# Mixer: residual base moved behind the scan and onto VectorE, out projection summed once; attention: the context's query and key norm moved ahead

## The chip, the cores and the metric

The kernel runs on one core of a Trainium2 chip. The metric is device time in microseconds (us) of one execution, the median of several runs. PE is TensorE, PEld its weight loads, DVE is VectorE, ACT ScalarE, POOL GpSimd and SP SyncE, which issues most DMAs.

## What is computed

The reference runs two networks of depth 2 on 512 tokens of width 1024, in fp32. The first one has in each layer a SwiGLU feed-forward net (FFN), a mixer and a second FFN; the second one has attention (grouped-query in layer 0, latent attention in layer 1, both with a context of 256 tokens) and an MLP. Cut to the parts that the change touches:

```
# mixer of layer l: three groups side by side, one out projection, a residual with layer norm
proj = h @ mix_w_in[l]                      # h = modulated x
y_ssd = mamba2_group(...)                   # 512 wide: conv, chunked scan, gate, group RMS norm
y_fox = fox_group(...)                      # 256 wide: forgetting attention
y_sc  = shortconv_group(...)                # 256 wide
y = concat([y_ssd, y_fox, y_sc]) @ mix_w_out[l]
x = layer_norm(ALPHA * x + gate * y, ln_g, ln_b)
# grouped-query attention: queries and keys of context and latents
q, k, v = split(h @ w_qkv)
q = rms_norm(q, q_norm); k = rms_norm(k, k_norm)    # the latents also get rope
```

## The kernel before

Tokens lie on the partitions for residuals (`z`, two tiles of 128 x 2 x 1024) and features on the partitions for what feeds a product. Every product is made of three fp32r matmuls on high and low parts (`mm3`): a value x is split into `hi` (cast by ACT) and `lo = x - hi` (DVE, or POOL where a piece of the plan says so). `WeightStream.fetch` (L288 to L304) loads a 512 KB block to one of three `raw` buffers by a DMA on SP, casts `hi` on ACT and subtracts `lo` on DVE, or in halves on POOL for the blocks in `onpool`. The blocks are taken in the order of `plan()`; at most five split pairs exist, three are fetched ahead, and a block in `extra` gets a place in the FFN's pool.

The tile framework simulates a timeline and orders each engine's instructions by it, with the order of the program as priority; on the chip every engine then runs its list in order. SBUF pools of consecutive phases share addresses: the mixer's pool `mx` and the attention's `gq` take the place of the FFN pool (`ff`), tile by tile as old tiles are released. PSUM has eight banks: tags "a" (two tiles of one bank), "b" (two tiles of two), "c" and "d" (one each).

**Mixer.** `mixer()` projects and convolves (`conv`, tiles `pxb` and `pxs`), and after the first four blocks calls `put_by`: that loads the layer norm's rows, lets POOL form the next residual base `ALPHA * (z * g + b)` in 4 scalings and 16 tensor operations of 128x512 (`next_base(..., True)`, L585 to L592) and then stores `z` to DRAM (`keep`). The scan and the forgetting attention follow. `out_first` (= `scan_out`) loads the base back and, while the gates, the short convolution and the group norm are computed, multiplies the FOX half `yq[0][:, 0:2]` by the first two blocks of `mo`, adding the gated result to `z` for each of eight 128x512 parts (L652, L654). After the mixer a phase with the FFN pool opens, and `out_chunk` multiplies the remaining 768 rows by six blocks and adds again, with the row sums for the layer norm (L652, L657). The low parts of all eight `mo` blocks are made by POOL.

**Attention.** `gqa_first` multiplies the context by the first four blocks of `w_qkv` while the norm of the latents still runs; its results stay in PSUM. In `gqa()` the generator `steps()` of head group 0 copies them to `gq`, takes squares, sums, `rsqrt`, gain (`norm(0)`), splits (`st`), transposes them (`turn`, tile `ptq`) and goes on with the projection of the latents (`dense(1, 0)`, `dense(1, 1)`, and so on), interleaved with the context's four heads.

Of the kernel before, what the change touches and what calls it, by code (L numbers as in the profile page):

```python
# [10 lines left out]
F32 = mybir.dt.float32  # L11
# [264 lines left out]
class WeightStream:  # L276
# [8 lines left out]
    def fetch(self):  # L285
        nc = self.nc
        src = self.plan[self.issued]
        n = src.shape[-1]  # L288
        self.issued += 1
        raw = self.pool.tile([P, DM], F32, tag="raw", bufs=self.raw_bufs, name="raw")  # L290
        if self.issued - 1 in self.extra:
            hi, lo = (self.extra_pool().tile([P, DM], F32R, tag="w" + i, bufs=1, name="w" + i) for i in "hl")
# [19 lines left out]
class Kernel:  # L312
# [526 lines left out]

    def mixer(self, l, h, put_by, out_first):  # L840
        nc, tc, ws = self.nc, self.tc, self.ws
        tt, stt, ts = nc.vector.tensor_tensor, nc.vector.scalar_tensor_tensor, nc.vector.tensor_scalar
        with tc.tile_pool(name="mx", bufs=1, reuse_waits="tile") as mp:
# [33 lines left out]

            put_by(lambda: T("le", 4, name="gb"))

# [291 lines left out]
    def softmax(self, ps, pool, pn, turn):  # L1171
# [100 lines left out]
    def gqa_first(self, hc):  # L1272

        w = [self.ws.next() for _ in range(4)]
        pb = self.ps("b", [P, CTB, SEQ], "pqkv")
        ps = [pb[:, tb, :384] for tb in range(CTB)]
        for tb in range(CTB):
            self.dense_tok(ps[tb], w, 2, 384, hc, range(KT), tb)
        return w, ps

    def gqa(self, h, hc, first, out_first):
# [4 lines left out]
        with tc.tile_pool(name="gq", bufs=1, reuse_waits="tile") as gp:  # L1286
# [4 lines left out]
            gain = gain[:, None].broadcast_to([P, 2, 5, 64])  # L1291
            yfc = self.xpool.tile([P, KT, CTX], F32, tag="lb", bufs=1, name="yfc")

            work = []

# [5 lines left out]
            def project(g):  # L1301
# [9 lines left out]

                def dense(b, i):
                    src, tb = (hc, 0) if b == 0 else (h, 2 * b - 2)
                    if i == 0:
                        tiles[b] = T("x", (P, 2, 5, 64)), T("t2", (P, 2, 5, 64))
                    x, sq = tiles[b]
                    v = out["v"][:, 2 * b + i]
                    if g == 0 and b == 0:
                        ps = first[1][i]
                    else:  # L1320
                        ps = self.ps("a" if g == 0 else "d", [P, 384], "pqkv")
                        self.dense_tok(ps, out["w"], 2, 384, src, range(KT), tb + i)
                    p5 = ps[:, 0:320].rearrange("p (h e) -> p h e", h=5)
# [3 lines left out]

                def norm(b):
                    x, sq = tiles[b]
                    tb = 2 * b - 2  # L1330
# [6 lines left out]
                    x10 = x.rearrange("p t h e -> p (t h) e")  # L1337
                    tt(x10, x10, r[:, :, None].broadcast_to([P, 10, 64]), op=ALU.mult)
                    st = tiles[b] = T("st", (P, 2, 6, P), 1, F32R)
                    dup = lambda i: st[:, :, i].rearrange("p t (a e) -> p t a e", a=2)  # L1340
# [19 lines left out]
                def steps():  # L1360
                    for b in range(3):
                        dense(b, 0)
# [16 lines left out]
            def head(g, q, out, ctx):  # L1379
# [9 lines left out]
                j = 2 * g + q // 2  # L1389
                return score, out["v"], yfc[:, j] if ctx else yf[j // 4][:, j % 4], (q % 2) * 64, t, nkb  # L1390

            def context_out(i):
                y = self.quads(1, CTX, "yc")[0]
                for j in range(4):
                    self.split(y[0][:, j], y[1][:, j], yfc[:, 4 * i + j], i == 0)
                return y

            def heads():
                out, steps = project(0)
                work.append(steps)  # L1400
                fill(6)
                for q in range(4):
# [195 lines left out]
    def plan(self):  # L1598
# [16 lines left out]
        def wide():  # L1615

            self.ws.extra.add(len(p))
# [15 lines left out]
        for l in range(DEPTH):  # L1633
# [21 lines left out]
    def run(self):  # L1655
        nc, tc, d = self.nc, self.tc, self.d
        with ExitStack() as es:
# [27 lines left out]
            self.ws = WeightStream(tc, wp, ahead=3, split_bufs=5, raw_bufs=3)  # L1685
            self.ws.extra_pool = lambda: self.fpool
            self.plan()
# [75 lines left out]
            for l in range(DEPTH):  # L1763
# [14 lines left out]

                def put_by(rows):

                    for n in range(2):
                        f = slice(n * SEQ, n * SEQ + SEQ)
                        gb = [rows(), rows()]
                        for i, x in enumerate(gb):
                            nc.sync.dma_start(x, d["rows"][1 + 3 * l, i][:, f])
                        self.next_base(old, SEQ, gb, f, True)
                    kept.append(keep(old))

                def scan_out(y, space):
                    z.extend(self.load_rows(kept[0], "z"))  # L1790
                    yield
                    self.ws.ahead = 2
                    gate = self.row(m1(1, 2), "c", space)
                    yield from self.out_steps([(z, gate, [y], SEQ)], (2,))

                yo, ys = self.mixer(l, h, put_by, scan_out)
# [4 lines left out]
                gate = self.row(m1(1, 2), "c")  # L1801
                self.out_chunk([(z, gate, [[a[:, 2:4] for a in yo], ys], SEQ)], (2, 4), True)
                h = norm(z, self.sums[0], SEQ, 2 + l * 3, m1(2, 0), m1(2, 1), 1e-5, f"md{l}1")
# [96 lines left out]
```

## Time and profile before

| | us |
|---|---|
| median of 3 runs | 3837.87 (3837.38 to 3838.32) |
| the profiled execution, its own time | 3839.17 |
| span of the profiled execution, first to last instruction | 3837.3 |
| TensorE busy within the span | 3637.5 (95%) |
| VectorE busy | 2529.1 (66%) |
| ScalarE busy | 1534.4 (40%) |
| GpSimd busy | 359.3 (9%) |
[...]

Two executions of the kernel before differ by up to some 0.02%. Busy times are unions over the instructions of an engine; a matmul's row shows more than its pace, since the next one starts before it ends. The mixer of layer 0 lies at some 412 to 640 us of the span and that of layer 1 at 1430 to 1650 us, the start of the grouped-query attention at 2045 to 2120 us.

### The profile page before, as it was taken

Reading aid. Unit: us, or ns where it says so; the run is one execution under the profiler, and the core shown is the slowest. Engines: PE = TensorE matmul, PEld = TensorE weight load, DVE = VectorE, ACT = ScalarE, POOL = GpSimd, SP = SyncE. Lnnn points to the kernel's source line nnn. Section 1 sums busy time; section 2 is a strip of 40 time slices with the busy share of each in tenths; the row PEclk is TensorE's granted clock in tenths of the full one; section 3 lists DMA queues with packets and bytes.
Section 4 is the critical chain, followed back from the end, with each engine's and each line's share of the span. In section 5 each row is a group of like instructions: output and inputs, shape, how many; then the busy total and the mean of one; then the engine's idle time right before and its main releaser. Section 6 shows DMA issues by size and latency. Waiting matters only on the chain. (4 is left out here: it accounts for less than half of the span.)

```text
span 3837.3 us, 49056 instructions
## 1 busy us (share of the span) xinstructions
PE 3637.5 (95%) x18970; PEld 3077.3 (80%) x18970; DVE 2529.1 (66%) x4245; ACT 1534.4 (40%) x2748; POOL 359.3 (9%) x388
## 2 busy tenths in 40 slices
PE   6999999999999999999998898999999979989998
PEld 5888777888888887778887787788888878878887
DVE  8775665777777966579665778664444558776454
ACT  3222443422332234452224566443232457644333
POOL 0000323000000004310001115100000001130000
PEclk9999999999999999999999899999999989999999
DMA  7663322566446633235642001122221210112222
GB/s 289 213 195 119 106 71 99 167 206 208 158 160 198 208 105 111 71 122 186 208 154 72 21 23 67 35 61 66 66 62 55 77 37 30 41 55 91 95 94 66
DMA packets 121738, 428.77 MB, mean 112 GB/s; under 512 B 13656, under 2 KB 19672, under 8 KB 119072
## 3 DMA queue, kind: packets, MB, share of 16 engines
q1 hardware_dynamic: 119584, 421.44, 33.7%
q10 hardware_dynamic: 1920, 4.19, 0.3%
q8 instruction: 149, 2.44, 0.3%
q14 instruction: 85, 0.70, 0.1%
HBM read 415.10 MB, written 10.49 MB: 111 GB/s over the span
## 5 line engine op out<-in xcount | busy, mean ns | idle before, releaser
L296 ACT CAST hi<-raw 128x1024 fp32r<-128x1024 f32 (+2 forms) x502 | 518.4, 1035 | 1314.4 <-PE pgu L348 726.6
L301 DVE TENSOR_TENSOR lo<-raw,hi 128x1024 fp32r<-128x1024 f32 (+2 forms) x472 | 577.0, 1224 | 337.5 <-ACT hi L296 333.8
L348 PE MATMUL pgu<-hl,hi 128*128 128x512 f32 (+1 forms) x1536 | 567.7, 370 | 4.5 <-DVE hl L530 2.9
L347 PE MATMUL pgu<-hh,hi 128*128 128x512 f32 (+1 forms) x1536 | 565.8, 370 | 5.7 <-ACT hh L621 3.3
L349 PE MATMUL pgu<-hh,lo 128*128 128x512 f32 (+1 forms) x1536 | 566.4, 369 | 0.0
L652 DVE TENSOR_TENSOR po<-po,gate 128x512 f32<-128x512 f32 x376 | 259.0, 696 | 357.6 <-PE po L349 357.6
L347 PE MATMUL po<-hi,gh 128*128 128x512 f32 x1216 | 474.4, 391 | 5.6 <-DVE z L654 3.1
L348 PE MATMUL po<-lo,gh 128*128 128x512 f32 x1216 | 472.8, 390 | 0.0
L349 PE MATMUL po<-hi,gl 128*128 128x512 f32 x1216 | 468.0, 389 | 0.0
L463 DVE SCALAR_TENSOR_TENSOR amul<-araw,crow 128x1024 f32<-128x1024 f32 x288 | 351.4, 1220 | 31.5 <-DMA araw<-in_ada 30.1
L348 PEld LDWEIGHTS pgu<-hl,hi 128*128 128x128 f32 x1536 | 292.8, 191 | 54.0 <-DVE hl L530 3.5
L347 PEld LDWEIGHTS pgu<-hh,hi 128*128 128x128 f32 x1536 | 291.4, 191 | 54.2 <-ACT hh L621 3.7
L349 PEld LDWEIGHTS pgu<-hh,lo 128*128 128x128 f32 x1536 | 292.9, 191 | 47.6 <-DVE lo L301 0.3
L347 PEld LDWEIGHTS po<-hi,gh 128*128 128x128 f32 x1216 | 228.4, 188 | 55.3 <-DVE z L654 5.6
L349 PEld LDWEIGHTS po<-hi,gl 128*128 128x128 f32 x1216 | 228.2, 188 | 47.8
L348 PEld LDWEIGHTS po<-lo,gh 128*128 128x128 f32 x1216 | 228.5, 188 | 45.1
L564 POOL TENSOR_TENSOR st<-st,mhalf 128x2 f32<-128x2 f32 (+2 forms) x24 | 19.9, 828 | 2601.9 <-DVE st L563 2601.9
L348 PE MATMUL pm<-hl,hi 128*128 128x512 f32 (+1 forms) x576 | 210.2, 366 | 2.0 <-DVE hl L622 2.0
L347 PE MATMUL pm<-hh,hi 128*128 128x512 f32 (+1 forms) x576 | 210.3, 367 | 1.9 <-ACT hh L621 1.6
L654 DVE TENSOR_TENSOR z<-po,z 128x512 f32<-128x512 f32 x304 | 206.5, 687 | 5.1
L349 PE MATMUL pm<-hh,lo 128*128 128x512 f32 (+1 forms) x576 | 209.5, 364 | 0.2 <-DVE lo L301 0.2
L333 DVE TENSOR_TENSOR gl<-gf,gh 128x512 fp32r<-128x512 f32 (+1 forms) x158 | 105.3, 668 | 115.7 <-ACT gh L331 115.0
(468 smaller groups left out, 7090.9 us busy)
## 6 DMA issues: line engine op xcount, KB each, us to landing
araw<-in_ada SPq DMA_DIRECT2D x224, 512.0 KB, 4.4
raw<-in_w SPq DMA_DIRECT2D x128, 512.0 KB, 3.5
raw<-in_f1i SPq DMA_DIRECT2D x88, 512.0 KB, 4.2
raw<-in_f2i SPq DMA_DIRECT2D x88, 512.0 KB, 3.8
raw<-in_mi SPq DMA_DIRECT2D x48, 512.0 KB, 3.5
raw<-in_f1o SPq DMA_DIRECT2D x44, 512.0 KB, 4.2
raw<-in_f2o SPq DMA_DIRECT2D x44, 512.0 KB, 4.4
arawf<-in_ada SPq DMA_DIRECT2D x16, 512.0 KB, 9.0
```

The costliest lines, as they stand in the source:

```text
L296: nc.scalar.copy(hi[:, :n], raw[:, :n])
L301: self.lo = nc.vector.tensor_tensor(lo[:, :n], raw[:, :n], hi[:, :n].bitcast(F32), op=ALU.subtract)
L333: ins = eng.tensor_tensor(lo, src, hi.bitcast(F32), op=ALU.subtract)
L347: mm(ps, ah, bh, start=start and i == 0, stop=False)
L348: mm(ps, ah, bl, start=False, stop=False)
L349: mm(ps, al, bh, start=False, stop=stop and i == n - 1)
L463: ins = nc.vector.scalar_tensor_tensor(m, w, 1.0, row, op0=ALU.mult, op1=ALU.mult, accum_out=res[:, j : j + 1])
L564: nc.gpsimd.tensor_tensor(r, sq, self.mhalf[:, :n], op=ALU.pow)
L652: nc.vector.tensor_tensor(ps, ps, gate[:, f], op=ALU.mult)
L654: nc.vector.tensor_tensor(to, ps, zf, op=ALU.add)
```

## The change

1. `put_by` now only stores `z`. `take_back`, called after the scan, loads `z` and four row tiles (in the scan's `le` buffers) and forms the base on DVE, in 16 operations of 128x512.
2. `out_first`, its gate row and its eight gated additions go. A new `mixer_out` multiplies all eight `mo` blocks into one accumulation for each of the eight parts: six parts (tags "b" and "a") take the FOX and short convolution halves, then each part its SSD half; the last two take everything after that. One gated addition each.
3. The low parts of the `mo` blocks and of four 128x512 pieces of `yq[0]` move from POOL to DVE. Blocks 4 to 7 of `mo` all get places in the FFN pool (tag "q4").
4. The short convolution's split now stands behind the group norms', whose four splits follow their own group.
5. `gqa_first` copies the context's queries and keys out of PSUM and norms them there, in the free tile `room`; `steps()` of group 0 is written out anew: the context's split, both projections of the first latent half, the context's transposes, and the products of the second half before its copies.

```diff
-    def mixer(self, l, h, put_by, out_first):
+    def mixer(self, l, h, put_by, take_back):
...
-            put_by(lambda: T("le", 4, name="gb"))
+            put_by()
...
-            work = out_first([a[:, 0:2] for a in yq[0]], T("vt", shape=(P, DM), name="gate"))
-            next(work)
+            base = take_back(lambda: T("le", 4, name="gb"))
+            next(base)
...
-                eng = nc.vector if g else nc.gpsimd
-                eng.tensor_tensor(lo, x, hi.bitcast(F32), op=ALU.subtract)
+                nc.vector.tensor_tensor(lo, x, hi.bitcast(F32), op=ALU.subtract)
...
-            group_norm(0)
-            group_norm(1)
+            yq += self.quads(1, SEQ, "my")
+            for g in range(2):
+                group_norm(g)
+                for j in range(2 * g, 2 * g + 2):
+                    split(1, j, xs[j])
             for j in range(2):
                 split(0, 2 + j, tmp[j])
-            yq += self.quads(1, SEQ, "my")
-            for j in range(4):
-                split(1, j, xs[j])
-            for _ in work:
+            for _ in base:
                 pass
+    def mixer_out(self, z, gate, yo, ys):
...
+        for part in range(2):
+            w += [self.ws.next() for _ in range(2)]
+            for tb, n in list(ps):
+                products(tb, n, part)
+        w += [self.ws.next() for _ in range(4)]
+        gate = self.row(gate, "c")
+        for tb in range(NTB):
+            for n in range(2):
+                if tb == NTB - 1:
+                    ps[tb, n] = self.ps("a", [P, SEQ], "po")
+                for part in range(0 if tb == NTB - 1 else 2, 4):
+                    products(tb, n, part)
...
+                nc.vector.tensor_tensor(p, p, gate[:, f], op=ALU.mult)
+                nc.vector.scalar_tensor_tensor(
+                    x, p, 1.0, x, op0=ALU.mult, op1=ALU.add, accum_out=self.sums[0][:, tb, n : n + 1]
+                )
...
     def gqa_first(self, hc):
...
+        x, sq = (cut(i * 640, i * 640 + 640).rearrange("p (t h e) -> p t h e", t=2, h=5) for i in range(2))
+        gain = cut(1280, 1600)
+        self.nc.sync.dma_start(gain, self.d["gqa_g"])
         for tb in range(CTB):
             self.dense_tok(ps[tb], w, 2, 384, hc, range(KT), tb)
+            p5 = ps[tb][:, 0:320].rearrange("p (h e) -> p h e", h=5)
+            self.nc.scalar.copy(x[:, tb], p5)
+            self.nc.scalar.activation(sq[:, tb], p5, AF.Square)
+        self.head_norm(x, sq, gain.rearrange("p (h e) -> p h e", h=5), lambda i: cut(1600 + 16 * i, 1610 + 16 * i))
...
+                    if g == 0:
+                        take(0, 0)
+                        take(0, 1)
+                        norm(0)
+                        dense(1, 0)
+                        dense(1, 1)
+                        for i in (2, 0, 1):
+                            turn(0, i)
+                        product(2, 0)
+                        product(2, 1)
+                        yield
+                        norm(1)
...
-            onpool(0, 8)
-            p.extend(d["mo"][l, i] for i in range(4))
-            wide()
-            p.extend(d["mo"][l, i] for i in range(4, 8))
+            for i in range(8):
+                if i > 3:
+                    wide()
+                p.append(d["mo"][l, i])
...
+                def take_back(rows):
...
+                    for n in range(2):
+                        for i in range(2):
+                            nc.sync.dma_start(gb[n][i], d["rows"][1 + 3 * l, i][:, n * SEQ : n * SEQ + SEQ])
+                    yield
...
+                            nc.vector.scalar_tensor_tensor(x, x, ALPHA, gb[n][0], op0=ALU.mult, op1=ALU.mult)
+                            nc.vector.scalar_tensor_tensor(x, gb[n][1], ALPHA, x, op0=ALU.mult, op1=ALU.add)
```

## Rows read from the trace of the kernel before

**Rows 1.** The page, busy time and share of the span.

```profile
PE 3637.5 (95%) x18970; PEld 3077.3 (80%) x18970; DVE 2529.1 (66%) x4245; ACT 1534.4 (40%) x2748; POOL 359.3 (9%) x388
```

**Rows 2.** Waits of PE, 405 to 700 us: total, times, longest.

```profile
PE pxs L347 <- ACT xbc L868: 4.5, 1, 4.5
```

**Rows 3.** Waits of PE, 1440 to 1720 us.

```profile
PE pxs L347 <- ACT xbc L868: 5.9, 1, 5.9
```

**Rows 4.** Timeline of DVE before the first wait: start, duration, instruction.

```profile
452.71 1.94 DVE L301 TENSOR_TENSOR lo<-raw,hi 128x1024 fp32r<-128x1024 f32 x1
...
454.81 1.07 DVE L907 TENSOR_TENSOR u<-u,sgn 128x48 f32<-128x48 f32 x1
455.91 1.20 DVE L908 SCALAR_TENSOR_TENSOR e<-u 128x48 f32<-128x48 f32 x1
457.14 0.19 DVE L919 TENSOR_SCALAR u<-u 128x48 f32<-128x48 f32 x1
```

**Rows 5.** Timeline of POOL, 423 to 462 us, its last row.

```profile
444.04 13.00 POOL L592 TENSOR_TENSOR z<-z,gb 128x512 f32<-128x512 f32 x8
```

**Rows 6.** Groups of DVE by line, 700 to 1000 us: busy, mean ns.

```profile
L301 DVE TENSOR_TENSOR lo<-raw,hi 128x1024 fp32r<-128x1024 f32 x56 | 68.4, 1222 | 37.4 <-ACT hi L296 37.4
```

**Rows 7.** Groups of DVE by line, 1446 to 1471 us.

```profile
L919 DVE TENSOR_SCALAR u<-u 128x48 f32<-128x48 f32 x1 | 1.2, 1165 | 0.0
```

**Rows 8.** Stretches: length, busy PE, PEld, DVE, ACT, POOL, PEclk, DMA.

```profile
461.40:466.70 5.30, 5.29 (x13) 4.14 (x14) 3.75 (x5) 1.89 (x3) 0.00 (x0) 0.50 0.47 116
...
1470.40:1474.00 3.60, 3.58 (x9) 2.88 (x10) 3.53 (x5) 1.27 (x2) 3.03 (x2) 0.53 0.20 26
622.50:638.90 16.40, 9.84 (x38) 5.98 (x36) 14.65 (x21) 5.34 (x8) 7.62 (x5) 1.00 0.22 64
...
1632.20:1648.50 16.30, 9.79 (x38) 5.96 (x36) 14.55 (x21) 5.29 (x8) 7.64 (x5) 1.00 0.20 63
...
588.00:622.50 34.50, 34.50 (x155) 27.84 (x154) 15.04 (x14) 15.92 (x23) 18.64 (x13) 1.00 0.20 63
```

**Rows 9.** Groups by line and shape, the whole span.

```profile
L652 DVE TENSOR_TENSOR po<-po,gate 128x512 f32<-128x512 f32 x376 | 259.0, 696 | 357.6 <-PE po L349 357.6
...
L654 DVE TENSOR_TENSOR z<-po,z 128x512 f32<-128x512 f32 x304 | 206.5, 687 | 5.1
...
L333 DVE TENSOR_TENSOR gl<-gf,gh 128x512 fp32r<-128x512 f32 x146 | 100.3, 688 | 113.2 <-ACT gh L331 113.1
```

**Rows 10.** Timeline of PE in the out projection: starts show the pace.

```profile
640.68 0.40 PE L348 MATMUL po<-lo,myh 128*128 128x512 f32 x1
640.91 0.39 PE L349 MATMUL po<-hi,myl 128*128 128x512 f32 x1
```

**Rows 11.** Timeline of ACT, 620 to 652 us.

```profile
634.61 1.14 ACT L1148 CAST myh<-xbc 128x512 fp32r<-128x512 f32 x2
...
645.30 1.05 ACT L296 CAST wh<-raw 128x1024 fp32r<-128x1024 f32 x1
```

**Rows 12.** Timeline of PE at the attention's start, 2074 to 2090 us.

```profile
2076.66 0.33 PE L348 MATMUL pqkv<-lo,hh 128*128 128x384 f32 x1
2076.84 0.33 PE L349 MATMUL pqkv<-hi,hl 128*128 128x384 f32 x1
...
2086.41 1.15 PE L1350 MATMUL ptq<-ident,st 128*128 128x128 f32 x4 [7.85 <-ACT st L331]
```

**Rows 13.** Timeline of ACT there.

```profile
2081.01 0.45 ACT L1324 COPY x<-pqkv 128x320 f32<-128x320 f32 x1
...
2085.96 1.02 ACT L331 CAST st<-x 128x256 fp32r<-128x256 f32 x3 [1.57 <-DVE x L1338]
```

**Rows 14.** Timeline of DVE there.

```profile
2082.98 0.82 DVE L1332 TENSOR_REDUCE r<-t 128x10 f32<-128x640 f32 x1 [0.83 <-ACT t L1325]
```

**Rows 15.** Stretch from that wait to the first latent head.

```profile
2078.50:2118.00 39.50, 25.14 (x138) 21.67 (x138) 29.66 (x67) 24.06 (x70) 10.44 (x19) 0.80 0.14 40
```

**Rows 16.** Timeline of PE, 2117 to 2119 us.

```profile
2117.86 0.63 PE L1387 MATMUL psc<-kth,qt 128*128 128x256 f32 x2
```

More of the change, by code (lines that the diff above doesn't have):

```diff
@@ L291, in fetch @@
         if self.issued - 1 in self.extra:
-            hi, lo = (self.extra_pool().tile([P, DM], F32R, tag="w" + i, bufs=1, name="w" + i) for i in "hl")
+            hi, lo = self.extra_pool()
         else:
@@ L1291, in gqa @@
             gain = gain[:, None].broadcast_to([P, 2, 5, 64])
-            yfc = self.xpool.tile([P, KT, CTX], F32, tag="lb", bufs=1, name="yfc")
-            work = []
+            work, own = [], {}
             def fill(n=1):
@@ L1312, in dense, with product, take @@
                 def dense(b, i):
+                    product(b, i)
+                    take(b, i)
+                def product(b, i):
                     src, tb = (hc, 0) if b == 0 else (h, 2 * b - 2)
+                    if g == 0 and b == 1:
+                        if i == 0:
+                            tiles["ps"] = self.ps("b", [P, CTB, SEQ], "pqkv")
+                        ps = tiles["ps"][:, i, :384]
+                    else:
+                        ps = self.ps("d" if g else "a", [P, 384], "pqkv")
+                    self.dense_tok(ps, out["w"], 2, 384, src, range(KT), tb + i)
+                    tiles["ps", b, i] = ps
+                def take(b, i):
+                    v = out["v"][:, 2 * b + i]
+                    if g == 0 and b == 0:
+                        ps = first[1][i]
+                        self.split(v[:, 0:64], v[:, 64:128], ps[:, 320:384])
+                        return
                     if i == 0:
@@ L1316, in dense @@
                     x, sq = tiles[b]
[L1317 to L1322, printed above, removed]
+                    ps = tiles["ps", b, i]
                     p5 = ps[:, 0:320].rearrange("p (h e) -> p h e", h=5)
@@ L1328, in norm @@
                 def norm(b):
+                    if g == 0 and b == 0:
+                        split(b, first[2])
+                        return
                     x, sq = tiles[b]
@@ L1338, in norm, with split @@
                     tt(x10, x10, r[:, :, None].broadcast_to([P, 10, 64]), op=ALU.mult)
+                    split(b, x)
+                def split(b, x):
                     st = tiles[b] = T("st", (P, 2, 6, P), 1, F32R)
@@ L1360, in steps @@
                 def steps():
-                    for b in range(3):
+                    if g == 0:
[10 more added lines that the diff above has]
+                        norm(1)
+                        take(2, 0)
+                        take(2, 1)
+                        yield
+                        for i in (2, 0, 1):
+                            turn(1, i)
+                        yield
+                        norm(2)
+                        yield
+                    for b in range(3 if g else 0):
                         dense(b, 0)
@@ L1389, in head @@
                 j = 2 * g + q // 2
-                return score, out["v"], yfc[:, j] if ctx else yf[j // 4][:, j % 4], (q % 2) * 64, t, nkb
+                if ctx and "yfc" not in own:
+                    own["yfc"] = self.xpool.tile([P, KT, CTX], F32, tag="lb", bufs=1, name="yfc")
+                return score, out["v"], own["yfc"][:, j] if ctx else yf[j // 4][:, j % 4], (q % 2) * 64, t, nkb
             def context_out(i):
@@ L1394, in context_out @@
                 for j in range(4):
-                    self.split(y[0][:, j], y[1][:, j], yfc[:, 4 * i + j], i == 0)
+                    self.split(y[0][:, j], y[1][:, j], own["yfc"][:, 4 * i + j], i == 0)
                 return y
@@ L1400, in heads @@
                 work.append(steps)
-                fill(6)
+                fill(1)
                 for q in range(4):
@@ L1685, in run, with place @@
             self.ws = WeightStream(tc, wp, ahead=3, split_bufs=5, raw_bufs=3)
-            self.ws.extra_pool = lambda: self.fpool
+            def place():
+                if self.wide:
+                    w = self.fpool.tile([P, 2, DM], F32R, tag="q4", bufs=4, name="wide")
+                    return w[:, 0], w[:, 1]
+                return (self.fpool.tile([P, DM], F32R, tag="w" + i, bufs=1, name="w" + i) for i in "hl")
+            self.wide, self.ws.extra_pool = False, place
             self.plan()
@@ L1777, in run, with put_by @@
                 old, z, kept = z, [], []
-                def put_by(rows):
+                def put_by():
+                    kept.append(keep(old))
+                def take_back(rows):
+                    z.extend(self.load_rows(kept[0], "z"))
+                    gb = [(rows(), rows()) for _ in range(2)]
+                    for n in range(2):
+                        for i in range(2):
+                            nc.sync.dma_start(gb[n][i], d["rows"][1 + 3 * l, i][:, n * SEQ : n * SEQ + SEQ])
+                    yield
+                    self.ws.ahead = 2
                     for n in range(2):
                         f = slice(n * SEQ, n * SEQ + SEQ)
[L1783 to L1796, printed above, removed]
+                        for tb in range(NTB):
+                            x = z[tb // 2][:, tb % 2, f]
+                            nc.vector.scalar_tensor_tensor(x, x, ALPHA, gb[n][0], op0=ALU.mult, op1=ALU.mult)
+                            nc.vector.scalar_tensor_tensor(x, gb[n][1], ALPHA, x, op0=ALU.mult, op1=ALU.add)
+                yo, ys = self.mixer(l, h, put_by, take_back)
                 if l == DEPTH - 1:
@@ L1800, in run @@
                 self.ws.ahead = 3
-                gate = self.row(m1(1, 2), "c")
-                self.out_chunk([(z, gate, [[a[:, 2:4] for a in yo], ys], SEQ)], (2, 4), True)
+                self.wide = True
+                self.mixer_out(z, m1(1, 2), yo, ys)
+                self.wide = False
                 h = norm(z, self.sums[0], SEQ, 2 + l * 3, m1(2, 0), m1(2, 1), 1e-5, f"md{l}1")
```

31 lines of the change are left out of this document (30 added, 1 removed).

## The prediction

> **What bounds the kernel now.** I read the page first: TensorE is busy in 95% of the span and no other engine in more than 66% [rows 1]. Time is therefore won where PE stands still or runs at its lower clock, and work taken from another engine counts only where PE waits for that engine. Then I listed PE's waits around the places that the diff touches. In the mixer of layer 0 the longest single wait is 4.5 us, for a convolution result [rows 2], and in layer 1 the same wait is 5.9 us [rows 3]; a table of stretches shows the granted clock at 0.50 and 0.53, the 1.2 GHz level, in the 5.3 and 3.6 us behind them [rows 8]. The second place is the first part of the out projection: of 16.40 us PE is busy in 9.84, of 16.30 in 9.79 [rows 8]. The third is the start of the attention, where PE stands 7.85 us before the first transpose of the context's keys [rows 12]. So there are three places, and each gets its own term.
>
> **Term A, the base leaves POOL.** PE's first wait ends with a chain on DVE, and that chain runs while POOL forms the base: POOL works without a break from 444.04 to 457.04 [rows 5]. In that time a subtraction of 128x1024 took 1.94 us and two operations on 48 columns took 1.07 and 1.20; 0.1 us after POOL is done, one of the same size takes 0.19 [rows 4], and the subtraction alone takes 1.222 on average of 56 [rows 6]. Without the POOL work the chain is shorter by 0.72 + 0.87 + 1.00 = 2.6 us in layer 0. In layer 1 the third small operation is slow too, 1.165 us [rows 7], so 3.6 there. The waits shrink to 4.5 - 2.6 = 1.9 and 5.9 - 3.6 = 2.3 us. The stretch at half clock costs 5.3 x 0.50 = 2.6 us and 3.6 x 0.47 = 1.7 us; whether a wait of 2 us still brings it is unknown. The nearest row is the out projection, with several short waits in 16.4 us and the clock at 1.00 throughout [rows 8], so I give both back. A = 2.6 + 3.6 + 2.6 + 1.7 = 10.5 us. Bounds: 0, if DVE's order changes so that the chain is as late as before, and 4.5 + 5.9 + 4.3 = 14.7, if the waits go altogether. [...]
>
> What the base costs in its new place: 16 DVE operations of 128x512 with operands in SBUF, at 0.69 us (the nearest rows are the subtraction of that size, 0.688, and the addition to z, 0.687 [rows 9]), together 11.0 us. They come after the scan. Four row tiles of 256 KB and the two loads of z go through SP's queue there, behind weight loads that wait for their buffers; the store of z goes ahead of the loads it used to follow. The cover is the stretch of 34.5 us in which PE is busy throughout with gates and short convolution and DVE in 15.0 [rows 8]. Without that cover DVE would hold the first gated addition by up to 11 us.
>
> **Term B, one accumulation.** PE's work stays: 48 + 144 = 192 matmuls before, 8 parts x 4 pieces x 6 = 192 after. What goes is the eight gated additions in between, 8 x (0.696 + 0.687) = 11.1 us of DVE per layer [rows 9], and with them the waits of PE for their PSUM tiles: six parts now start in six banks with nothing to wait for. I give back the idle time of both stretches, 6.56 + 6.51 = 13.1 us [rows 8]. DVE gets the low parts of eight blocks (8 x 1.222 = 9.8 us [rows 6]) and four splits (2.8 us), so in the 51 us from 588 to 639 it does about 15.0 + 14.7 - 8 (additions gone from there) + 11.0 + 9.8 + 2.8 = 45 us: nearly full, not over. What can come late is the FFN pool. Blocks 4 to 7 lie there, in addresses of the mixer's last tiles, and every part needs them after the first 72 matmuls. At 0.23 us each [rows 10] these take 16.6 us, so PE, free for them at 622.5 [rows 8] and with the group norm's product and the changes of part ahead, needs the blocks at some 641; the last casts of the group norm's result ended at 635.75 [rows 11] and should come some us sooner without the additions in their way. I charge 1 us of new waiting per layer, between 0 and the 12.7 of the rival below. B = 13.1 - 2 = 11.1 us.
>
> **Term C, the context's norm.** The chain that PE awaits for 7.85 us starts with the first copy at 2081.01, on ACT, and reaches the splits at 2085.96 [rows 13]: copies, squares, a sum of 0.82 us [rows 14], rsqrt, gain, product. Moved into `gqa_first` it runs under the norm of the latents, where both products are long in PSUM; the addition to POOL's and DVE's queues there is one gain multiplication and some 3 us, and to SP's one load of the gains. The splits can then start some 4 us sooner, at about 2082. Meanwhile PE has the second latent block's projection, 24 matmuls at 0.175 us [rows 12], 4.2 us, which fills from 2078.6 to 2082.8. The hole is thereby closed, and the latents' projections, which came after it, move up; their norms set the first latent head, now at 2117.86 [rows 16]. How much of it arrives there? At least the 4 us of the splits, unless DVE holds it (then 0). At most: DVE was busy in 29.7 of the 39.5 us [rows 15] and loses 3 of that, so 39.5 - 26.7 = 12.8. I take the middle of 4 and 12, C = 8 us, since PE's 25.1 busy us there [rows 15] hold several at a clock of 0.80 that get faster too.
>
> **The sum.** 10.5 + 11.1 + 8 = 29.6 us. The profiled execution took 3839.2 us, which makes 3809.6. It was 1.3 us slower than the median of the runs, 3837.87, so against the median 3808.
>
> **The rivals.**
> - *The blocks in the FFN pool come late.* Before, the one block placed there was cast only at 645.30 [rows 11]. If all four start then, the second is ready at 645.3 + 1.05 + 2 x 1.22 = 648.8, against 641.3 when PE arrives, and the fourth, whose load must wait for a raw buffer, some 2 us after PE needs it: 9.3 us, and 3.4 us for a stretch at half clock as in layer 0's first wait. That is 12.7 per layer, 23.4 more than charged: 3831, no measurable change. For it speaks that row; against it, that the row stands behind a cast which waited for the old first part's products.
> - *DVE's order keeps the chains.* The convolution chain stays at its place in A (only the clock is won, 4.3) and DVE binds the attention's start (C = 2): 4.3 + 11.1 + 2 = 17.4, which is 3820. For it: DVE is 75% busy there [rows 15].
> - *VectorE takes over the end of the mixer, slower.* The base's rows land late, its 11 us run after the group norm's splits, and the casts of blocks 4 to 7, which need the row tiles' addresses, start only when it is done. Started at 650, PE loses 12.2 + 1.9 + 3.4 = 17.5 per layer, 33 more than charged: 3841. Each us later costs two; from 653 on the kernel is slower by over 0.2%. Place: PE's entry into the SSD half. For it: DVE's 45 us of work in 51. Against it: DVE is only 44% busy from 588 to 622 [rows 8], where the base fits.
> - *More than forecast.* Both convolution waits go, and C is 12: 14.7 + 13.1 + 12 = 39.8, 3798; with the shorter wait at the FFN's start some us less, 3794.
>
> **How the numbers follow.** A change of 0.2% (7.7 us) can be told from none. Forecast 0.60 (3796 to 3818), more than it 0.05, DVE's order 0.15, late blocks 0.13 (a quarter of it still faster), VectorE as the bound 0.07. Faster: 0.60 + 0.05 + 0.15 + 0.03 = 0.83; same 0.10; slower 0.07. The range from 3794 to 3831 leaves out less than 2 in 10 and ends at the late blocks.
>
> **What would show it.** A: no POOL work between the convolutions, subtractions at 1.22 us, PE's wait before `pxs` under 2.5 us, and the clock at 1.00 behind it. B: `po` in one run of 72 matmuls without a wait for z, then no wait for `wh` or lo parts above 1 us. C: `ptq` within 1 us of the projections, and the first latent head at about 31 us behind the last transposes of the norm. Wrong it would be if PE waits for a cast or a low part at the SSD half, if the gated additions wait for the base, or if the convolution wait stays although POOL is idle.

## The result, and the profile after

The changed kernel takes 3797.61 us (median of 4 runs, 3793.83 to 3799.79); the kernel before took 3838.10 beside it (4 runs). The ratio is 0.9891, with a 95% interval from 0.9878 to 0.9905. That is 40.5 us won where 30 were forecast. The profiled execution after took 3799.79 us, its span is 3798.0, so the two spans differ by 39.3 us. Executions of one kernel lie further apart than the 0.02% that three runs suggested: the four of the kernel before go from 3837.4 to 3843.2, nine of `c_alone` (below) from 3823.0 to 3836.1.

The page's busy times first: PE keeps nearly all its work, POOL loses a third of its own [rows 1].

```profile
PE 3630.7 (96%) x18954; PEld 3074.0 (81%) x18954; DVE 2517.9 (66%) x4269; ACT 1532.4 (40%) x2744; POOL 237.7 (6%) x308
```

Then PE's waits from 405 to 700 us (total, times, longest). The wait before `pxs` is 0.7 us instead of 4.5 [rows 2]; in layer 1 the same line stands, 0.7 instead of 5.9 [rows 3]. The lines for `ptf` (transposes in the scan's last steps) and `prow` (transposes that form the gate row) are new. No line for `po`, the out projection, is left.

```profile
PE ptf L1051 <- DVE pn L1227: 1.0, 1, 1.0
PE pxs L347 <- ACT xbc L868: 0.7, 1, 0.7
...
PE prow L404 <- DVE xbc L1136: 0.4, 1, 0.4
```

DVE's timeline ahead of that wait shows the chain without POOL beside it: the subtraction takes 1.22 us instead of 1.94, and the two small operations 0.21 each instead of 1.07 and 1.20 [rows 4].

```profile
450.31 1.22 DVE L301 TENSOR_TENSOR lo<-raw,hi 128x1024 fp32r<-128x1024 f32 x1
...
451.68 0.21 DVE L907 TENSOR_TENSOR u<-u,sgn 128x48 f32<-128x48 f32 x1
451.92 0.21 DVE L908 SCALAR_TENSOR_TENSOR e<-u 128x48 f32<-128x48 f32 x1
```

Four stretches (columns as in [rows 8]): behind the convolution wait the clock is at 1.00, two stretches inside the scan are at half clock (0.51 and 0.50; in the second one matmuls of 512 columns start 0.43 us apart, 1.2 columns per ns, as in the stretch that the prediction calls the 1.2 GHz level; the pace in [rows 10] is 0.23), and from the short convolution's end PE is busy without a gap for 43.2 us, where it was busy 9.84 of 16.40 before.

```profile
455.80:472.00 16.20, 15.28 (x83) 13.10 (x83) 10.93 (x14) 6.93 (x10) 0.00 (x0) 1.00 0.25 69
...
505.70:509.10 3.40, 3.31 (x10) 2.75 (x11) 3.34 (x8) 0.87 (x3) 0.07 (x1) 0.51 0.14 54
526.20:529.60 3.40, 3.40 (x9) 2.64 (x9) 2.06 (x7) 1.53 (x5) 0.00 (x0) 0.50 0.06 23
...
619.80:663.00 43.20, 43.20 (x193) 35.41 (x192) 29.61 (x52) 16.70 (x22) 0.71 (x1) 1.00 0.43 153
```

PE's timeline at the attention's start: the context's transposes follow the projection's matmuls at once, where PE stood 7.85 us [rows 12].

```profile
2060.37 0.34 PE L349 MATMUL pqkv<-hi,hl 128*128 128x384 f32 x1
2060.55 0.60 PE L1426 MATMUL ptq<-ident,st 128*128 128x128 f32 x4
...
2087.04 0.50 PE L1483 MATMUL psc<-kth,qt 128*128 128x256 f32 x2 [0.52 <-DVE kth L1429]
```

To see where 39.3 us come from I cut PE's timeline at first and last matmuls: "conv" is from the first `pxb` to the end of `pxs`, "scan" from there to the first `pz`, "end" from there to the second FFN's first `pgu`, "attn" all of `pqkv` in the first attention, "last" from the first `psc` of the last attention to the first `pm`. All times are us, two numbers are layers 0 and 1. "Split" is the longest split of `yql` (a low part of the attention's result) on VectorE in "last"; most take 0.69. The experiments below are in the same table; times are medians, stages are of the one profiled execution.

```
kernel        time     conv         scan           end          attn    last   split
before        3838.1   63.6, 63.8   111.2, 112.8   91.6, 91.6   299.1   318.5   8.24
after         3797.6   57.0, 57.0   115.7, 115.7   83.0, 83.0   287.5   315.2   5.58
after_again   3796.2   57.0, 57.0   112.5, 114.2   83.0, 83.0   289.8   315.2   5.59
c_alone       3829.7   63.2, 63.7   111.2, 112.8   91.6, 91.6   292.8   313.8   1.67
no_c          3808.9   57.0, 57.0   114.2, 114.2   83.0, 83.0   302.6   318.6   8.26
base_only     3827.3   57.0, 57.0   114.2, 114.2   91.0, 91.0   297.8   318.6   8.29
base_pool     3804.1   63.8, 62.8   112.8, 112.9   83.0, 83.0   286.3   312.3   3.25
pool_scalar   3793.4   57.4, 57.4   112.5, 112.5   83.0, 83.0   288.6   315.4   5.65
no_base       3791.0   57.0, 57.0   114.4, 111.2   83.0, 83.0   287.7   313.1   3.36
base_twice    3803.2   57.0, 57.0   114.8, 113.1   83.0, 83.0   289.1   318.6   8.27
base_behind   3791.2   57.0, 57.0   112.8, 111.2   83.0, 83.0   288.3   313.1   3.39
behind_again  3791.9   57.0, 57.0   112.9, 111.2   83.0, 83.0   288.2   313.2   3.43
low_pool      3794.5   57.0, 57.0   112.5, 112.5   83.0, 83.0   289.6   315.3   5.60
mla_dve       3800.3   57.0, 57.0   114.2, 115.7   83.0, 83.0   286.3   318.6   0.77
```

Before to after: conv -13.4, scan +7.4, end -17.2, attn -11.6, last -3.3, all the rest -1.2; together -39.3. So the mixer's end gave more than forecast, the convolutions gave back half in the scan, and 3.3 us come from a place that no edit touches.

### The profile page after: what moved, and what is told of

Its sections match the earlier page's. It is cut to its first block, busy times and chain, and to the rows that moved or that the text cites. A ratio compares the mean times of both kernels' runs of the same rounds, so it can differ in the third digit from the quotient of the medians.

```text
span 3798.0 us, 48955 instructions
## 1 busy us (share of the span) xinstructions
PE 3630.7 (96%) x18954; PEld 3074.0 (81%) x18954; DVE 2517.9 (66%) x4269; ACT 1532.4 (40%) x2744; POOL 237.7 (6%) x308
## 5 line engine op out<-in xcount | busy, mean ns | idle before, releaser
L296 ACT CAST hi<-raw 128x1024 fp32r<-128x1024 f32 (+1 forms) x496 | 511.6, 1034 | 1292.3 <-PE pgu L348 706.4
L301 DVE TENSOR_TENSOR lo<-raw,hi 128x1024 fp32r<-128x1024 f32 (+1 forms) x480 | 578.0, 1206 | 351.8 <-ACT hi L296 347.7
L652 DVE TENSOR_TENSOR po<-po,gate 128x512 f32<-128x512 f32 x344 | 236.9, 697 | 325.1 <-PE po L349 324.9
L654 DVE TENSOR_TENSOR z<-po,z 128x512 f32<-128x512 f32 x288 | 195.6, 688 | 4.9
```

Of the source, the lines that this page charges most:

```text
L652: nc.vector.tensor_tensor(ps, ps, gate[:, f], op=ALU.mult)
L654: nc.vector.tensor_tensor(to, ps, zf, op=ALU.add)
```

## The experiments

### The parts by themselves

**c_alone** and **no_c** do or undo the attention part (`gqa_first`, `head_norm`, `gqa`) as a whole.

> The kernel before with the attention part of the change alone (context norm in gqa_first, the new order of steps, yfc taken later). Theory: the gain of this part is independent of the mixer; the changed kernel came out 11.6 us better across the first attention, so 3838.1 - 11.6 = 3826.5, with the 7.85 us wait before the context's first transposes gone and the waits of 4.5 and 5.9 us for the convolutions kept. Whether the last attention is 3.3 us shorter too, as in the changed kernel, is open: if it is, 3823. Rival 1: the forecast's 8 us, 3830. Rival 2: most of the 11.6 us needs the mixer's new order ahead of it; then 3834 or more.

> The changed kernel with the attention part undone. Theory: it loses the 11.6 us of the first attention and nothing else, 3797.6 + 11.6 = 3809.2. Rival: the 3.3 us of the last attention, which no edit touches, hang on this part as well; then 3812.5. Second rival: the parts overlap and undoing this one costs less than 8 us, below 3805.6.

With the part alone the kernel takes 3829.7 us, with it undone 3808.9: 8.5 and 11.3 us. The nine runs of `c_alone` lie from 3823.0 to 3836.1, so they cannot tell the theory's 3826.5 from the first rival's 3830; they speak against the second rival's 3834. For `no_c` the theory's number held (3809.2), but not its sum: the profiled execution was the slowest of five (3813.3), and in it "attn" is 15.1 us longer than in the changed kernel, "last" 3.4 longer and "scan" 3.0 shorter. The last attention is short with the part here and long without it, 313.8 and 318.6; but `base_twice` has the part and 318.6, so it doesn't hang on it (more below). In `no_c` the wait is back, 8.1 us long:

```profile
PE ptq L1389 <- ACT st L331: 9.4, 2, 8.1
```

The windows over the whole "attn" stage tell why the two differ (length, PE busy, granted clock): kernel before, then `no_c`, `c_alone` and the changed kernel:

```profile
2048.60:2347.70 299.10, 262.63 (x1649) 241.70 (x1648) 217.26 (x477) 184.45 (x463) 42.66 (x73) 0.94 0.10 32
```

```profile
2020.50:2323.10 302.60, 265.48 (x1649) 243.78 (x1648) 217.84 (x477) 184.59 (x463) 42.65 (x73) 0.93 0.10 32
```

```profile
2047.80:2340.70 292.90, 262.11 (x1649) 241.09 (x1648) 217.44 (x477) 184.53 (x464) 42.94 (x73) 0.95 0.10 33
```

```profile
2024.60:2312.10 287.50, 257.79 (x1649) 237.21 (x1648) 217.16 (x477) 184.60 (x463) 42.75 (x73) 0.96 0.10 34
```

PE's idle time (length less busy) is 36.5 and 37.1 us without the part, 30.8 and 29.7 with it: 5.7 to 7.4 us of waiting go in either pair. The same 1649 matmuls are busy for 257.8 to 265.5 us, at a clock of 0.96 to 0.93; the rest of the difference is in this busy time, which is longer where the mean clock is lower.

**base_only** moves the base alone and keeps the two-part out projection; **base_pool** undoes that move alone.

The edit of `base_only`, in `put_by` and `scan_out` of the kernel before, cut to its main lines; `base_pool` takes the same move back in the changed kernel:

```diff
-                        self.next_base(old, SEQ, gb, f, True)
...
                     self.ws.ahead = 2
...
+                            nc.vector.scalar_tensor_tensor(x, x, ALPHA, gb[n][0], op0=ALU.mult, op1=ALU.mult)
+                            nc.vector.scalar_tensor_tensor(x, gb[n][1], ALPHA, x, op0=ALU.mult, op1=ALU.add)
                     gate = self.row(m1(1, 2), "c", space)
```

> The kernel before with the base late on VectorE alone; the out projection in two parts and the attention as before. Theory: the convolution waits shrink to 0.72 us in both layers (6.2 and 6.8 us won by the end of pxs), and 4.1 and 2.9 us of it are given back in the scan; the base itself is done before the first gated addition. 3838.1 - 6.0 = 3832. Rival 1: without the cover of a longer accumulation the first gated addition waits for the base, up to 11 us in each layer: 3838 or more. Rival 2: nothing is given back in the scan: 3825.

> The changed kernel with the mixer's base formed by POOL between the convolutions as before; the one accumulation and the attention part stay. Theory: the waits of 4.5 and 5.9 us before pxs are back, with the half clock behind them, and the small waits and half-clock stretches that the changed kernel has in the scan go, so the net loss is the 2.1 + 3.9 = 6.0 us read off the two traces: 3803.6. Rival 1: nothing was given back for this reason; then the forecast's 10.5 us, 3808.1. Rival 2: not POOL's work but DVE's order made the waits; then they stay away though POOL is busy, 3797.6.

`base_only` takes 3827.3: 11.0 us won, near the forecast's 10.5 and between theory and second rival. Of the 11.8 us in its profile "conv" and "scan" together give 9.0; the rest lies in the later stages. "Conv" is 57.0 in both layers, so the convolution waits need nothing but the base's move. The first gated addition doesn't wait 11 us: the base is done in time under the old out projection too, whose waits are 6.4 us in all, as in the kernel before:

```profile
PE po L347 <- DVE z L654: 5.2, 5, 1.6
...
PE po L347 <- DVE scv L1003: 1.2, 1, 1.2
```

`base_pool` takes 3804.1, within 0.5 us of the theory, which is in part luck: against the changed kernel its profile has 12.6 us more in "conv", 5.7 less in "scan", as the theory says, but also 4.1 less in the two attentions, for which the theory has nothing. PE's list has the old wait in both layers, in the same words (in layer 1 the kernel before has 5.9):

```profile
PE pxs L347 <- ACT xbc L868: 4.5, 1, 4.5
```

and DVE's timeline has the slow operations again, among them two that the prediction's rows begin too late to show, the subtractions at 441.49 and 448.75:

```profile
441.49 1.66 DVE L301 TENSOR_TENSOR lo<-raw,hi 128x1024 fp32r<-128x1024 f32 x1
...
448.75 1.40 DVE L301 TENSOR_TENSOR lo<-raw,hi 128x1024 fp32r<-128x1024 f32 x1
...
452.95 1.94 DVE L301 TENSOR_TENSOR lo<-raw,hi 128x1024 fp32r<-128x1024 f32 x1
...
455.04 1.07 DVE L907 TENSOR_TENSOR u<-u,sgn 128x48 f32<-128x48 f32 x1
456.14 1.20 DVE L908 SCALAR_TENSOR_TENSOR e<-u 128x48 f32<-128x48 f32 x1
```

`base_only` and `no_c` differ by the one accumulation (with its low parts and splits), and so do `c_alone` and `base_pool`: 18.3 us in the one pair and 25.5 in the other. "End" alone is shorter by 16.0 and 17.2; the rest lies in other stages, the attentions above all, which this edit does not touch.

### What it takes to hold VectorE

**pool_scalar** is the changed kernel with 22 multiplications by one on POOL, of a tile that nothing else reads, in `put_by`:

```diff
+                    g = rows()
+                    nc.sync.dma_start(g, d["rows"][1 + 3 * l, 0][:, :SEQ])
+                    for _ in range(22):
+                        nc.gpsimd.tensor_scalar(g, g, 1.0, None, op0=ALU.mult)
```

> The changed kernel with POOL kept busy between the convolutions by 22 multiplications of 128x512 by one, in place on a tile that nothing else reads (one SBUF input each, 22 x 1.47 = 32 us, as long as the base's run was). It asks whether POOL's mere traffic makes VectorE's operations late or the base in particular (its loads, its store, its place). Theory: any work of POOL on SBUF does it; the wait before pxs is above 3 us in both layers and the time rises by 3 to 9 us, 3801 to 3807. Rival: it takes POOL operations with two SBUF inputs; the wait stays at 0.72 and the time at 3797.6.

The theory fell. POOL is busy throughout the convolutions, and yet most of DVE's operations there take nearly their usual times (of the six subtractions from 438 to 460 us five take 1.21 or 1.22 us and one 1.61, and the four small operations behind them 0.20 to 0.59); PE's wait before `pxs` is 1.2 us, and the time is 2.8 us below that of the changed kernel run beside it (3796.2). POOL's row, then DVE's:

```profile
429.22 38.66 POOL L1887 TENSOR_SCALAR gb<-gb 128x512 f32<-128x512 f32 x22 [10.24 <-DMA gb<-in_rows]
```

```profile
451.80 1.22 DVE L301 TENSOR_TENSOR lo<-raw,hi 128x1024 fp32r<-128x1024 f32 x1
...
453.17 0.38 DVE L907 TENSOR_TENSOR u<-u,sgn 128x48 f32<-128x48 f32 x1
453.58 0.21 DVE L908 SCALAR_TENSOR_TENSOR e<-u 128x48 f32<-128x48 f32 x1
```

Here it is POOL's operations that come out longer: most of the 22 take 1.49 us, but six take 1.69 to 2.58, each beside a subtraction of VectorE. So POOL's being busy is not enough to make the chain slow. What it takes instead is not shown, for three things differ from the base's run. Its tensor operations read two SBUF inputs, `z` and the rows. They follow each other without a gap, while here each multiplication reads what the one before wrote and starts 0.08 us behind it. And three of the four row loads are left out here. The number of inputs alone does not decide: in `base_pool` a split of 128x512 on VectorE that starts inside a one-input scaling takes 0.97 us, where the changed kernel has 0.69.

```profile
426.53 1.49 POOL L585 TENSOR_SCALAR gb<-gb 128x512 f32<-128x512 f32 x1
```

```profile
426.71 0.97 DVE L622 TENSOR_TENSOR hl<-hf,hh 128x512 fp32r<-128x512 f32 x1 [5.59 <-ACT hh L621]
```

### What the base costs in its new place

**no_base** leaves the 16 operations out and **base_twice** runs over `n in (0, 1, 0, 1)`, so neither computes what the reference does; **base_behind** orders each first operation of a piece behind the scan's last copy. **behind_again** is that kernel a second time, beside **after_again**, the changed kernel itself. The edit of `base_behind`:

```diff
-                    nc.vector.tensor_copy(y, tmp["y"])
+                    self.scanned = nc.vector.tensor_copy(y, tmp["y"])
...
-                            nc.vector.scalar_tensor_tensor(x, x, ALPHA, gb[n][0], op0=ALU.mult, op1=ALU.mult)
+                            self.after(nc.vector.scalar_tensor_tensor(x, x, ALPHA, gb[n][0], op0=ALU.mult, op1=ALU.mult), self.scanned)
```

> The changed kernel without the 16 operations that form the base (z is taken back as it was stored; rows are still loaded). Theory: 11 us of VectorE's work in each layer are hidden but for the waits of 0.41 and 0.95 us which they put into the scan's last steps, and these go: 3797.6 - 2 x 1.36 = 3795. The half-clock stretches in the scan stay, since the earlier pxs brings them and not the base. Rival: the base also brought the half clock there; then 3795 - 3.7 = 3791. Second rival: wholly hidden, 3797.6.

> The changed kernel with the 16 operations of the base done twice (another 11 us of VectorE in each layer, in the same place). It asks how much room VectorE had at the mixer's end. Theory: it is busy in 31.5 of 51 us from 588 to 639, so another 11 us fit under the gates; only the wait in the scan's last steps may grow by one operation of 0.69: 3797.6 to 3799. Rival, the forecast's third: VectorE takes over, the gated work and the low parts of the wide blocks come late, and the 11 us cost at least 5 in each layer: 3808 or more.

> The changed kernel with the base ordered behind the copy of the scan's last result, so that none of its operations stands ahead of the last normalisation in VectorE's queue. Theory: the waits of 0.41 and 0.95 us go in both layers, and the 11 us still fit: 3797.6 - 2.7 = 3795. Rival: the base now holds the group norm's chain, which VectorE does next, and PE waits for it at the last two products: 3797.6 or more.

> The changed kernel itself, as a control beside the next three. Every theory: 3797.6 within 3 us. Its stages from the first gate to the end of the mixer and its last attention show how much of the difference between kernels is there without any edit.

> The changed kernel with the base ordered behind the scan's last copy, once more beside the changed kernel itself. Theory: of the 6.4 us that it was faster in another call, 2.7 come from the edit (the waits of 0.41 and 0.95 us in both layers), the rest from half-clock stretches and from the last attention, which the edit only shifts: 2.7 to 6.4 us faster than the control, 3791 to 3795. Rival: all of it was chance, and the two agree within 1 us.

DVE's timeline of the changed kernel shows the place: base operations stand ahead of the last normalisation of the scan (`pn`), for which PE waits.

```profile
582.79 0.68 DVE L1900 SCALAR_TENSOR_TENSOR z<-gb,z 128x512 f32<-128x512 f32 x1
583.38 0.49 DVE L1227 TENSOR_SCALAR pn<-pn,sm 128x512 f32<-128x512 f32 x1
583.93 3.10 DVE L1899 SCALAR_TENSOR_TENSOR z<-z,gb 128x512 f32<-128x512 f32 x5
```

Without the base, and with it ordered behind, PE's wait before `ptf` is gone and that before `prow` falls from 0.41 us to 0.14 at most; with the base doubled the longer one is 1.6 instead of 1.0. The "scan" column is then the same sum in every kernel that was run: 111.2, plus 1.3 if the base stands there (1.95 doubled), plus 1.6 for each half-clock stretch inside. Of these stretches the changed kernel's profile had two in each layer, its second one none and one, and the kernel before none and one; what brings them is not shown. The windows over layer 0's scan, of `after` and of `after_again`, show the same work at two clocks:

```profile
468.60:584.30 115.70, 112.17 (x637) 85.32 (x636) 74.52 (x151) 52.56 (x110) 20.51 (x16) 0.97 0.24 76
```

```profile
469.00:581.50 112.50, 108.97 (x638) 82.96 (x637) 74.11 (x150) 52.62 (x110) 20.53 (x16) 1.00 0.23 78
```

So of the 7.4 us given back in the scan 2.6 are the base's place, and 4.8 are half-clock stretches which the next execution has not. `no_base` took 3791.0, the number of its rival, but the base does not bring the half clock: without it layer 0 has two such stretches and layer 1, with the same code, none (114.4 and 111.2).

VectorE's room is real: doubled, the base costs 0.6 us more in each layer and nothing in "end". The median of `base_twice` is 5.6 us higher all the same. Its four runs are 3798.8, 3799.2, 3807.2 and 3810.7 us; the profile is of the one at 3799.2, whose "last" is 3.4 longer and whose "scan" is 3.5 shorter than the changed kernel's, and what made the other two slow is not shown. Ordering the base behind wins 4.3 us beside its control, 2.6 of it the edit's in "scan"; 3791.2, and 3791.9 when repeated, are the least times of all kernels here that leave no work out. The first of them is 3.8 us under its theory, the repetition within its own.

### The low parts

**low_pool** sends them to POOL, in `plan` of the changed kernel:

```diff
+            onpool(0, 8)
             for i in range(8):
```

> The changed kernel with the low parts of all eight blocks of the out projection on POOL (as the kernel before had them; there the last four were narrow blocks, but for one). Theory: the low parts are off PE's path on VectorE; on POOL the three of the FFN pool that are cast by 632 take 2 x 1.25 us each, 630.6 + 7.5 = 638.1, where PE reaches the first at 636.2 and the third some 2.8 us later, so PE waits for less than 1 us in each layer: 3797.6 to 3800. Rival: VectorE, freed of 9.8 us per layer, brings the gated work sooner: 3795 or less. Second rival: POOL's run holds VectorE's operations as in the convolutions, and the group norm comes late: above 3801.

It takes 3794.5, and "end" is 83.0 as in every kernel with one accumulation: PE waits for no low part on either engine, where the theory gave less than 1 us of waiting, and neither rival's way is seen, though the first's number is. The median is 1.7 us below the control's, and the runs of the two overlap; in the profiles one half-clock stretch in layer 1's scan makes 1.7 (114.2 there, 112.5 here). POOL's operations have two SBUF inputs here, but PE's list shows no new wait for VectorE beside them.

### The last attention

Where do 3.3 us come from that no edit touches? In the kernel before, a split on VectorE falls into POOL's run of the last base; POOL's row, then VectorE's:

```profile
3379.74 9.88 POOL L592 TENSOR_TENSOR z<-z,gb 128x512 f32<-128x512 f32 x8
```

```profile
3381.92 8.24 DVE L333 TENSOR_TENSOR yql<-yf,yqh 128x512 fp32r<-128x512 f32 x1
```

In the changed kernel it starts later in POOL's last run, of seven operations:

```profile
3324.63 5.87 POOL L585 TENSOR_SCALAR gb<-gb 128x512 f32<-128x512 f32 x4 [34.57 <-DMA gb<-in_rows]
...
3344.99 8.72 POOL L592 TENSOR_TENSOR z<-z,gb 128x512 f32<-128x512 f32 x7
```

```profile
3348.68 5.58 DVE L333 TENSOR_TENSOR yql<-yf,yqh 128x512 fp32r<-128x512 f32 x1
```

Both end 0.55 us behind POOL's last instruction (3389.62 and 3390.16; 3353.71 and 3354.26). PE waits behind them, 7.1 us before and 3.9 after; the lists are of the kernel before and the changed one:

```profile
PE pyo L1235 <- DVE pt L333: 8.0, 3, 7.1
```

```profile
PE po L347 <- DVE z L654: 4.2, 2, 3.9
```

**mla_dve** forms that base on VectorE, in `out_first` of the last attention:

```diff
-                    self.next_base(z, SEQ, (gb[:, 0], gb[:, 1]), pool=True)
...
+                                self.late(nc.vector.scalar_tensor_tensor(x, x, ALPHA, gb[:, 0, f], op0=ALU.mult, op1=ALU.mult))
+                                nc.vector.scalar_tensor_tensor(x, gb[:, 1, f], ALPHA, x, op0=ALU.mult, op1=ALU.add)
```

> The changed kernel with the base of the last attention on VectorE in place of POOL (16 operations of 128x512 and no multiplication of the rows by the factor ahead). Theory: the 3.3 us that the change won in the last attention came from where a split of 128x512 fell: it took 8.24 us in the kernel before and 5.58 in the changed one, and both times it ended 0.55 us behind the last instruction of POOL's run. Without POOL's run it takes 0.69, PE's wait of 3.91 us behind it falls below 1 us and the half clock there goes too: 3797.6 - 3 to 5 = 3793 to 3795. Rival: VectorE is busy in 15.3 of each 20 us there, the 16 x 0.69 = 11.0 us more come onto PE's path, and the time is the same or up to 3803.

The split does as the theory says, and the gain isn't there. The longest `yql` split is 0.77 us; but VectorE takes seven and eight base operations in a row, and PE has a wait of 5.6 us that it had not, for the softmax:

```profile
3321.08 4.90 DVE L1950 SCALAR_TENSOR_TENSOR z<-z,gb 128x512 f32<-128x512 f32 x8 [0.29 <-DMA gb<-in_rows]
...
3327.31 4.28 DVE L1951 SCALAR_TENSOR_TENSOR z<-gb,z 128x512 f32<-128x512 f32 x7
```

```profile
PE pkn L347 <- ACT pn L1218: 5.6, 1, 5.6
```

At 3800.3 it is 2.7 us above the changed kernel, within the rival's "the same or up to 3803". In the table's other kernels, which leave this place alone, "last" goes with the split: 8.2 to 8.3 us with 318.5, 5.6 with 315.3, 3.4 or less with 312.3 to 313.8. Kernels that have the same code in this place get different ones, so edits ahead of it move where the split falls; how they do it was not followed.

## Why the prediction was right

The direction, the three places and the range held. The gain came out a third larger than the sum, and its parts differ from the forecast's: in the profiled pair A gave 4.5 us less, B 6.1 more, C 3.6 more, the last attention 3.3 and the rest 1.2 that were not in the sum. That these errors partly cancel is luck; the time lies 3.6 us above the range's lower end.

**Term A, forecast 10.5.** The mechanism, a VectorE chain that is slow beside the base's POOL run, was right; which property of that run does it stays open (see `pool_scalar`). The waits fell further than worked out, to 0.72 us where 1.9 and 2.3 were given, because the chain was late before the first row that was counted: VectorE reaches it at 452.71, in the changed kernel at 450.31, and of these 2.4 us only 0.9 are the stage's own later start. Waits and clock together gave 13.4 in "conv" against 10.5. The step that failed is the cover of the base: it does hold VectorE's 11 us, but the base starts early enough to stand ahead of the scan's last normalisation, 2.6 us which were costed at nothing. 13.4 - 2.6 = 10.8 is the term; the whole of `base_only` measured 11.0. In the profiled pair it is only 6.0, since three more half-clock stretches of the scan fell on the changed kernel's side; `base_pool` costs 6.5 in time and 6.9 in "conv" and "scan".

**Term B, forecast 11.1, measured 17.2 in "end".** The idle time went as said, but for 1.0 us per layer before the norm's transposes, and the 1 us charged for the wide blocks never came: three of their four low parts are done at 634.1, and PE reaches the first block at 636.2 and waits for none. What was mis-sized is "PE's work stays". The matmuls do, but the gate row is formed once instead of in each part (4 transposes in the stage instead of 12), and the 192 `po` matmuls take 1.8 us less (46.48 to 44.71), mostly since the 30 between the waits from 622.5 to 638.9 took 8.28 us, 0.28 each and not the pace of 0.23. Windows over the whole stage, of before and of after, give PE 2.75 us less work and 5.85 us less idle:

```profile
587.30:678.90 91.60, 84.71 (x379) 66.70 (x377) 51.74 (x76) 33.87 (x48) 32.02 (x23) 1.00 0.30 104
```

```profile
584.30:667.30 83.00, 81.96 (x371) 66.69 (x369) 55.37 (x89) 33.80 (x47) 3.29 (x3) 1.00 0.39 133
```

**Term C, forecast 8, measured 11.6.** The idle part was 6.8 us (5.7 to 7.4 between pairs), so the term was sized well for the waiting; 4.8 us are PE's busy time (262.6 to 257.8), at a mean clock of 0.96 and not 0.94. But its sign was not met: the latents' scores came 35.0 us behind the norm's last transposes (2052.0 to 2087.0) and not 31, against 39.3 before. Windows over that stretch, before and after, show that PE's idle time fell by 7.3 us there, and that 12 more matmuls came into it:

```profile
2078.60:2117.90 39.30, 24.97 (x137) 21.57 (x138) 29.66 (x67) 23.96 (x70) 10.44 (x19) 0.80 0.14 41
```

```profile
2052.00:2087.00 35.00, 27.93 (x149) 25.10 (x148) 27.80 (x62) 22.81 (x66) 9.00 (x18) 0.80 0.15 46
```

So 4.3 us were won by that point as the prediction counts it, 2.6 ahead of the stretch and 4.7 behind it, where the mean clock is 0.98 and was 0.95.

**The rivals.** Late blocks, VectorE at the mixer's end and DVE's order all failed: no wait for `wide`, room for twice the base, and chains that moved up. The time is that of "more than forecast", 3798, but not by its way: A gave less than it says, B more, and 3.3 us came from a place it doesn't name. The 3.4 us that two rivals charge for the half clock of layer 0's first wait are shown by no run: term A reads 2.6 for the same stretch, and those inside the scan cost 1.6 each. It changes no verdict.

## What to carry to other kernels

Look at which POOL operations run before you blame POOL for being busy: here a run of tensor operations without gaps, with two SBUF inputs each, made VectorE's operations up to 1 us longer in the convolutions (1.20 instead of 0.21 us, 2.13 instead of 1.22), and a spaced chain with one input hardly did (0.38 instead of 0.21, one subtraction 1.61); which of the two differences counts was not separated. When work goes to an engine with room, order it behind the last thing for which the bounding engine waits; that was worth 2.6 us here, and the room alone did not give it. Compare stage by stage, profile the unchanged kernel twice, and note which execution a profile is of (for `no_c` it was the slowest of five): half-clock stretches and one split's place moved single stages by 1.6 to 6 us without an edit there.

## What was not expected of the hardware

A VectorE split of 128x512 that starts inside POOL's run of two-input operations ended 0.55 us after the run's end, in the kernel before and the changed one, and took 8.24 and 5.58 us instead of 0.69. In twelve of the thirteen profiles in which POOL forms that base the longest split took 3.25 to 8.29 us; in `no_c` (8.26) and `base_pool` (3.25), too, it ended 0.54 and 0.56 us behind such a run. In `c_alone`, where it falls among the products ahead of that run, it took 1.67 us, and in the convolutions VectorE's slow operations took 1.07 to 2.15 us, though POOL's run there went on for 13 us and more. What makes the difference was not tried and stays open.
